# Experts of a two-layer trunk in chunks of 1024 columns: longer DMA rows, one split per load, 11 load buffers

## The chip, the cores and the metric

The kernel runs on one core of a Trainium2 chip. The metric is device time in microseconds (us) of one execution, the median of several runs. PE is TensorE (matmuls), PEld its weight loads, DVE is VectorE, ACT is ScalarE, POOL is GpSimd and SP is SyncE, which issues most transfers.

## The reference, cut to what matters

Two layers act on 256 tokens of width 1024: attention and a SwiGLU, then an HGRN2 mixer and a layer of experts. Only the experts change:

```python
def moe_swiglu(u, w_router, w_gate, w_up, w_down):
    t = u.reshape(B * S, D)                       # 256 x 1024, normalised
    logits = (t @ w_router).astype(F32)
    top_vals, top_idx = lax.top_k(logits, TOP_K)  # 2 of 8
    top_w = jax.nn.softmax(top_vals, axis=-1)
    gates = jnp.sum(jax.nn.one_hot(top_idx, N_EXPERTS, dtype=F32) * top_w[..., None], axis=1)
    out = jnp.zeros((B * S, D), F32)
    for e in range(N_EXPERTS):
        y = swiglu(t, w_gate[e], w_up[e], w_down[e]).astype(F32)
        out = out + gates[:, e:e + 1] * y
```

`swiglu` is `(silu(t @ w_gate) * (t @ w_up)) @ w_down`, with 3584 hidden columns per expert. All weights are float32: 44 MB for each expert, 352 MB of the 427 MB that the kernel reads.

## The kernel before

Products are made in a float32 format of reduced precision, so each operand is split into two parts, and a product is three matmuls: high x high, high x low, low x high (`mm3`, lines 101 to 103). Activations are split once per stage. Weights are split as they come: `load` (L83) takes a buffer of the pool `raws` (14 buffers of 1 MB) and issues one transfer on SP's queue; `split` (L88) makes `w_hi` on ACT by a copy and `w_lo` on DVE by a subtraction, into the pool `subs` (four buffers of each, 1024 columns wide). A load is split twice, by halves. The tile framework orders the instructions of each engine and puts in the waits; the order on an engine is fixed at build time.

The stages are attention (to 130 us), SwiGLU (to 340), HGRN2 (to 494) and the experts (to 1501). At the experts' start the tokens are normalised and transposed in two parts (`dense`), a router product of 24 small matmuls gives the logits (`route`, L1010), and DVE finds the two experts of each token (`sel`), its gate (`gw`) and its place in the list of each expert (`place`), for one token tile of 128 after the other. PE helps with sums over tokens (`pp`, L1036). `nh` and `nl` are the normalised tokens in two parts.

Each expert works on up to 128 tokens, gathered by a product with one-hot matrices (`one_hot`, L1053, `gather_pair`, L1060) for two experts at a time, e = 0, 2, 4, 6. An expert is seven jobs of 512 hidden columns. A job has a `gate` and an `up` (two loads each, 2 KB per row, 24 matmuls each), `hm` = the product of silu(gate) and up (L1111, DVE), a `turn` (four transposes, L1116, and the split of the result into `hh` on ACT and `hl` on DVE, L1120 and L1121) and a `down` (two loads of 4 KB rows, 24 matmuls into `pj`). `run_jobs` (L1208) interleaves them: gate of a job, turn of the one before, up, down of the one before. After an expert's last job `scatter` (L1194) multiplies the rows back to their tokens (L1202, L1203) and adds them to `h` (L1204). `FirstJob` runs its gate over all 256 tokens, 48 matmuls, while routing is under way; the result is gathered afterwards. `LastJob` ends half of the columns before the other, so that the output can leave early.

After all jobs the kernel counts the tokens of the fullest expert (L1254 to L1260); if there are more than 128, a second pass (L1262) does the rest. With these inputs it does not run, but the value has to be loaded by each engine (L1261) and the branch taken.

## Time and profile before

| | us |
|---|---|
| median of 3 runs | 1511.85 (1510.98 to 1514.09) |
| profiled execution, span | 1509.5 |
| of it, up to the first `up` matmul of the experts | 518.1 |
| of it, from there to the end of the last `down` matmul | 981.2 |
| of it, after that | 10.2 |
| PE busy | 1476.0 |
| DVE busy | 1243.6 |
| ACT busy | 1042.5 |

The span runs from the first to the last instruction that the profiler recorded in one execution. Busy time of an engine counts its own instructions; where an engine is busy almost all the time, the question is what it does and where its few gaps are, so the timeline and the waits matter more than the shares. The experts take the same pattern 56 times over, so one chunk's length times the number of chunks is most of the time. TensorE's granted clock was full through the experts.

### The profile page before, as it was taken

Reading aid. Unit: us, or ns where it says so; the run is one execution under the profiler, and the core shown is the slowest. Engines: PE = TensorE matmul, PEld = TensorE weight load, DVE = VectorE, ACT = ScalarE, POOL = GpSimd, SP = SyncE. Lnnn points to the kernel's source line nnn. Section 1 sums busy time; section 2 is a strip of 40 time slices with the busy share of each in tenths; the row PEclk is TensorE's granted clock in tenths of the full one; section 3 lists DMA queues with packets and bytes.
Section 4 is the critical chain, followed back from the end, with each engine's and each line's share of the span. In section 5 each row is a group of like instructions: output and inputs, shape, how many; then the busy total and the mean of one; then the engine's idle time right before and its main releaser. Section 6 shows DMA issues by size and latency. Waiting matters only on the chain.

```text
span 1509.5 us, 20242 instructions
## 1 busy us (share of the span) xinstructions
PE 1476.0 (98%) x7573; PEld 1228.3 (81%) x7573; DVE 1243.6 (82%) x1474; ACT 1042.5 (69%) x1293; POOL 14.9 (1%) x32
## 2 busy tenths in 40 slices
PE   7999999999999999999999999999999999999997
PEld 6787899998888788888888878888777887887885
DVE  7775655566767899999899998898889889889886
ACT  6655544445656788878778877777777777777774
POOL 1000000000000000000000000000000000000000
...
GB/s 312 368 117 112 137 185 195 178 185 182 140 156 125 142 376 363 373 364 362 360 325 377 377 329 362 371 315 362 362 369 345 361 355 326 362 363 343 365 260 31
DMA packets 208683, 429.85 MB, mean 285 GB/s; under 512 B 7290, under 2 KB 58530, under 8 KB 208578
## 3 DMA queue, kind: packets, MB, share of 16 engines
...
q8 instruction: 61, 1.00, 0.3%
...
## 4 chain that ended last, share of the span: by engine, by line
PE 92%; DVE 3%; ACT 2%; issue 1%; DMA 1%; POOL 0%; SPq 0%; ACTq 0%; DVEq 0%; POOLq 0%
PE acc L102 17%; PE acc L101 17%; PE acc L103 16%; PE pj L103 8%; PE pj L102 8%; PE pj L101 8%; PE pj L342 3%; PE pj L344 3%; PE pj L343 3%; DVE w_lo L91 2%; PE tp L1116 1%; PE pj L759 1%; PE pj L760 1%; PE pj L761 1%; PE acc L1069 1%
## 5 line engine op out<-in xcount | busy, mean ns | idle before, releaser
L91 DVE TENSOR_TENSOR w_lo<-raw,w_hi 128x1024 fp32r<-128x1024 f32 x810 | 958.5, 1221 | 163.4 <-ACT w_hi L91 146.1
L91 ACT ACTIVATE w_hi<-raw 128x1024 fp32r<-128x1024 f32 x810 | 835.8, 1058 | 275.8 <-PE acc L103 101.9
L102 PE MATMUL acc<-w_lo,xgh 128*128 128x512 f32 x904 | 357.2, 395 | 0.9
L101 PE MATMUL acc<-w_hi,xgh 128*128 128x512 f32 x904 | 355.9, 394 | 1.0 <-ACT xgh L294 1.0
L103 PE MATMUL acc<-w_hi,xgl 128*128 128x512 f32 x904 | 353.1, 391 | 0.0
L102 PEld LDWEIGHTS acc<-w_lo,xgh 128*128 128x128 f32 x904 | 169.7, 188 | 50.3 <-DVE w_lo L91 14.5
L101 PEld LDWEIGHTS acc<-w_hi,xgh 128*128 128x128 f32 x904 | 169.8, 188 | 36.4 <-ACT xgh L294 1.2
L103 PEld LDWEIGHTS acc<-w_hi,xgl 128*128 128x128 f32 x904 | 169.7, 188 | 33.8
L102 PE MATMUL pj<-w_lo,hh 128*128 128x512 f32 x448 | 177.1, 395 | 0.3
L103 PE MATMUL pj<-w_hi,hl 128*128 128x512 f32 x448 | 174.6, 391 | 0.3
L101 PE MATMUL pj<-w_hi,hh 128*128 128x512 f32 x448 | 161.1, 391 | 2.2 <-ACT hh L1120 1.7
L101 PEld LDWEIGHTS pj<-w_hi,hh 128*128 128x128 f32 x448 | 84.1, 188 | 21.5 <-ACT hh L1120 2.7
L102 PEld LDWEIGHTS pj<-w_lo,hh 128*128 128x128 f32 x448 | 84.1, 188 | 18.2 <-DVE w_lo L91 1.6
L103 PEld LDWEIGHTS pj<-w_hi,hl 128*128 128x128 f32 x448 | 84.1, 188 | 17.5 <-DVE hl L1121 1.1
L342 PE MATMUL pj<-xh,w_hi 128*128 128x256 f32 x320 | 90.8, 284 | 0.6 <-DVE hm L676 0.6
L344 PE MATMUL pj<-xh,w_lo 128*128 128x256 f32 x320 | 90.6, 283 | 0.0
L343 PE MATMUL pj<-xl,w_hi 128*128 128x256 f32 x320 | 90.6, 283 | 0.0
L1106 ACT ACTIVATE sg<-acc 128x512 f32<-128x512 f32 x55 | 33.0, 599 | 46.7 <-PE acc L103 46.7
L342 PEld LDWEIGHTS pj<-xh,w_hi 128*128 128x128 f32 x320 | 61.4, 192 | 1.2 <-DVE hm L676 0.8
L343 PEld LDWEIGHTS pj<-xl,w_hi 128*128 128x128 f32 x320 | 61.4, 192 | 0.4
L344 PEld LDWEIGHTS pj<-xh,w_lo 128*128 128x128 f32 x320 | 61.4, 192 | 0.0
L1120 ACT ACTIVATE hh<-tp 128x512 fp32r<-128x512 f32 x56 | 33.3, 595 | 40.4 <-PE pj L102 33.2
...
## 6 DMA issues: line engine op xcount, KB each, us to landing
...
```

Source lines behind the costliest of these rows:

```text
L91: split.last = nc.scalar.activation(hi, view, AF.Copy), nc.vector.tensor_sub(lo, view, f32(hi))
L101: nc.tensor.matmul(ps, lhsT=xh, rhs=wh, start=first, stop=False, skip_group_check=chk)
L102: nc.tensor.matmul(ps, lhsT=xh, rhs=wl, start=False, stop=False, skip_group_check=chk)
L103: nc.tensor.matmul(ps, lhsT=xl, rhs=wh, start=False, stop=last, skip_group_check=chk)
L342: nc.tensor.matmul(o, lhsT=wh[:, i, j], rhs=xh[:, k], start=k == 0 and j == 0, stop=False, skip_group_check=True)
L343: nc.tensor.matmul(o, lhsT=wh[:, i, j], rhs=xl[:, k], start=False, stop=False, skip_group_check=True)
L344: nc.tensor.matmul(o, lhsT=wl[:, i, j], rhs=xh[:, k], start=False, stop=k == KT - 1, skip_group_check=True)
L759: nc.tensor.matmul(o, lhsT=wh[:, k], rhs=xh[:, k], start=first, stop=False, skip_group_check=True)
L760: nc.tensor.matmul(o, lhsT=wh[:, k], rhs=xl[:, k], start=False, stop=False, skip_group_check=True)
L761: nc.tensor.matmul(o, lhsT=wl[:, k], rhs=xh[:, k], start=False, stop=last, skip_group_check=True)
L1106: nc.scalar.activation(self.sg, ps, AF.Silu)
L1120: nc.scalar.activation(self.hh, ptv, AF.Copy)
```

## The change

Experts are worked in jobs of 1024 columns, three per expert and one of 512 (the first of expert 0, the last of the others). A gate or up load covers two k-tiles of 1024 columns, in rows of 4 KB; a down load covers a pair of neighbouring hidden rows per partition, 8 KB, so the hidden columns of a job are permuted: `hm` is written (L1201) with even and odd columns apart, and the transposes read it so. Each load is one `Group` with one split of 128x2048 on ACT and one on DVE, and 12 matmuls. Splits are made three groups ahead (three `w_hi`, two `w_lo` buffers of a new pool `parts`), loads eleven ahead. The pool `subs` stays for the earlier stages only and is freed with them, and `parts` takes its place. The tables that route tokens were rewritten (`one_hot`, `pick`) to allow half-size lists, a form that the constant TWO = False leaves out; what stays of it are more table operations on DVE at the start and a transposition against an `order` matrix instead of the identity. The count of the fullest expert is made in `route`. The diff, cut to its core:

```diff
-NRAW = 14
+NRAW = 11
 NSUB = 4
+TWO = False
...
-    subs = ctx.enter_context(tc.tile_pool(name="subs", bufs=NSUB))
...
+    subs = early.enter_context(tc.tile_pool(name="subs", bufs=NSUB))
...
-    moe = ctx.enter_context(tc.tile_pool(name="moe", bufs=2))
+    moe = ctx.enter_context(tc.tile_pool(name="moe", bufs=1))
     mc = ctx.enter_context(tc.tile_pool(name="mc", bufs=1))
-
-    def slot_tiles(n):
-        """transposed rows in two parts: [feature, k-tile, row]"""
-        return [xgs.tile([P, KT, n], F32R, name=nm, tag=nm) for nm in ("xgh", "xgl")]
+    parts = ctx.enter_context(tc.tile_pool(name="parts", bufs=1))
...
+    lower = mc.tile([P, P], F32R, name="lower")
+    nc.vector.tensor_scalar(lower, ident, 0.0, None, op0=ALU.mult)
+    nc.vector.tensor_copy(lower[:, 0:HS], ident[:, HS:P])
+
+
+    even = mc.tile([P, P], F32, name="even")
+    nc.gpsimd.iota(it.rearrange("p (a b) -> p a b", b=2), pattern=[[1, HS], [0, 2]], base=1, channel_multiplier=0)
+    nc.vector.tensor_copy(even, it)
+    nc.vector.memset(even[:, 1:P:2], 0.0)
+    nc.vector.tensor_sub(even, even, slot1)
+    twice = mc.tile([P, P], F32, name="twice")
+    nc.vector.memset(twice[:, 0:HS], 0.0)
+    nc.vector.memset(twice[:, HS:P], -float(HS))
+
+    pi = moe.tile([P, 1], I32, name="pi", tag="pi")
+    nc.gpsimd.iota(pi, pattern=[[0, 1]], base=1, channel_multiplier=1)
+    place1 = mc.tile([P, 1], F32, name="place1")
+    nc.vector.tensor_copy(place1, pi)
+    step = mc.tile([P, 1], F32, name="step")
+    nc.vector.tensor_scalar(step, place1, float(HS), -float(P - 1), op0=ALU.is_gt, op1=ALU.mult)
+    nc.vector.scalar_tensor_tensor(step, place1, -1.0, step, op0=ALU.add, op1=ALU.add)
...
+            if t == NT - 1:
+                pc = bank("tp")
+                for u in range(NT):
+                    nc.tensor.matmul(pc[:, 0:NE], lhsT=ones, rhs=sel[:, u], start=(u == 0), stop=(u == NT - 1))
+                nc.vector.tensor_copy(count, pc[:, 0:NE])
+                if TWO:
+                    nc.vector.tensor_scalar(few, pc[:, 0:NE], float(HS), None, op0=ALU.is_le)
+                else:
+                    nc.vector.memset(few, 0.0)
+                nc.vector.tensor_reduce(out=cmax_i, in_=count, axis=AX.X, op=ALU.max)
...
+    def one_hot(e, small_slots, name):
+
+        slots = moe.tile([P, 2, P], F32, name="slots", tag="slots")
+        for i in range(2):
+            nc.vector.scalar_tensor_tensor(slots[:, i], small_slots, few[:, e + i:e + i + 1], slot1, op0=ALU.mult, op1=ALU.add)
+        oneh = moe.tile([P, NT, 2, P], F32R, name=name, tag=name, bufs=2)
         for t in range(NT):
-            nc.vector.tensor_tensor(out=oneh[:, t], in0=slot1[:, None, :].to_broadcast([P, 2, P]),
-                                    in1=place[:, t, e:e + 2, None].to_broadcast([P, 2, P]), op=ALU.is_equal)
+            nc.vector.tensor_tensor(out=oneh[:, t], in0=slots, in1=place[:, t, e:e + 2, None].to_broadcast([P, 2, P]),
...
+    class Group:
+
+        def __init__(self, pieces, arm, n):
+            self.pieces, self.arm, self.n = pieces, arm, n
+
+        def load(self):
+            self.raw = load([2048], self.pieces)
+
+        def split(self):
+            self.hi = parts.tile([P, 2048], F32R, name="w_hi", tag="w_hi", bufs=3)
+            self.lo = parts.tile([P, 2048], F32R, name="w_lo", tag="w_lo", bufs=2)
+            nc.scalar.activation(self.hi, self.raw, AF.Copy)
+            nc.vector.tensor_sub(self.lo, self.raw, f32(self.hi))
...
+            self.wd = weights[2].rearrange("(r p i) c -> p r (i c)", p=P, i=2)
...
+                return Group(lambda r: [(r.rearrange("p (k c) -> p k c", k=nk), w[:, k0:k0 + nk, self.c0:self.c0 + width])],
+                             arm, self.n)
+
+            return [begin] + [group(k0) for k0 in range(0, KT, nk)] + [lambda: self.low(box)]
...
+        def upped(self):
+
+            self.fold(self.pu)
+            self.hm = moe.tile([P, self.nb, 2, 2, P], F32, name="hm", tag="hm")
+            for b in range(self.nb):
+                nc.vector.tensor_mul(self.hm[:, b].rearrange("s a i p -> s a p i"),
+                                     self.pu["ps"][b].rearrange("s (a p i) -> s a p i", a=2, i=2),
+                                     self.sg[:, b].rearrange("s (a p i) -> s a p i", a=2, i=2))
...
+                return Group(lambda r: [(r, self.wd[:, self.c0 // 256 + a, :])], arm, self.n)
+
+            return [begin] + [group(a) for a in range(2 * self.nb)] + ([self.out] if self.last else [])
...
+    def run_jobs(jobs, fresh=lambda job: None):
+
+        todo = []
         prev = None
         for job in jobs + [None]:
-            if job and job.fresh:
-                job.fresh(job.shared)
-                if prev:
-                    prev.turn()
-                    prev.down()
-                    prev = None
+            into, rest = [], []
             if job:
-                job.gate()
+                into, rest = job.gate(), job.up()
+                rest[2:2] = [job.gated]
+                more = fresh(job)
+                if more:
+                    todo += more[:2] + ([prev.upped] if prev else []) + more[2:] + ([prev.turn] if prev else []) + into
+                elif prev:
+                    todo += into[:2] + [prev.upped] + into[2:] + [prev.turn]
+                else:
+                    todo += into
+                todo += rest
+            elif prev:
+                todo += [prev.upped, prev.turn]
             if prev:
-                prev.turn()
-            if job:
-                job.up()
-            if prev:
-                prev.down()
+                todo += prev.down()
             prev = job
 
+        groups = [i for i in todo if isinstance(i, Group)]
+        loaded = split_ = at = 0
+        for i in todo:
+            if isinstance(i, Group):
+                while split_ < min(at + 3, len(groups)):
+                    while loaded < min(split_ + NRAW, len(groups)):
+                        groups[loaded].load()
+                        loaded += 1
+                    groups[split_].split()
+                    split_ += 1
+                at += 1
+            i()
...
+    def pick(e, sh):
+        def fn():
+
+            sh["pick"] = one_hot(e, even, "low")
+            sh["oneh"] = one_hot(e, twice, "oneh")
+            for i in range(2):
+                at = small.tile([P, 1], F32, name="at", tag="at")
+                nc.vector.scalar_tensor_tensor(at, step, few[:, e + i:e + i + 1], place1, op0=ALU.mult, op1=ALU.add)
+                sh["order", i] = moe.tile([P, P], F32, name="order", tag="order", bufs=3)
+                nc.vector.tensor_scalar(sh["order", i], slot1, at, None, op0=ALU.is_equal)
+
+        return fn
...
+        widths = (1, 2, 2, 2) if e == 0 else (2, 2, 2, 1)
...
-    pc_ = bank("tp")
-    nc.tensor.matmul(pc_[:, 0:NE], lhsT=ones, rhs=sel[:, 0], start=True, stop=False)
-    nc.tensor.matmul(pc_[:, 0:NE], lhsT=ones, rhs=sel[:, 1], start=False, stop=True)
-    cmax = mc.tile([P, 1], F32, name="cmax")
-    nc.vector.tensor_reduce(out=cmax, in_=pc_[:, 0:NE], axis=AX.X, op=ALU.max)
-    cmax_i = mc.tile([P, 1], I32, name="cmax_i")
-    nc.vector.tensor_copy(cmax_i, cmax)
```

On DVE, where the previous stage ends, stood before, with the splits of the experts' first load (`raw_4991`) ahead of `ol`, the last part of the HGRN2 mixer, and `h0`, the residual:

```order
L915 TENSOR_TENSOR og_4746<-tp_4735,sg_4685 128x512
L916 TENSOR_TENSOR og_4746<-og_4746,hss_4748 128x512
L91 TENSOR_TENSOR w_lo_4994<-raw_4991,w_hi_4993 128x1024
L91 TENSOR_TENSOR w_lo_5010<-raw_4991,w_hi_5009 128x1024
L931 SCALAR_TENSOR_TENSOR ol_4772<-tp_4766,cols_88,oh_4771 128x512
```

and there now stands:

```order
L916 TENSOR_TENSOR og_4746<-tp_4735,sg_4685 128x512
L917 TENSOR_TENSOR og_4746<-og_4746,hss_4748 128x512
L932 SCALAR_TENSOR_TENSOR ol_4772<-tp_4766,cols_88,oh_4771 128x512
L310 TENSOR_TENSOR h0_77<-acc_3466,h0_77 128x512
L310 TENSOR_TENSOR h0_77<-acc_3467,h0_77 128x512
```

The two splits have gone from there.

Further on in DVE's order, at the routing, stood before (`nl` are the low parts of the tokens, `lT` and `lg` the logits, `m8` and `ix` the top two; `w_lo_5028` and `w_lo_5044` belong to the second load):

```order
L294 TENSOR_TENSOR xgl_4830<-tp_4878,xgh_4829 128x4x128
L1051 SCALAR_TENSOR_TENSOR nl0_4978<-hg0_4827,rs_4836,nh0_4900 128x512
L91 TENSOR_TENSOR w_lo_5028<-raw_5025,w_hi_5027 128x1024
L1051 SCALAR_TENSOR_TENSOR nl1_4983<-hg1_4828,rs_4863,nh1_4901 128x512
L1016 COPY lT_4930<-pj_4905 8x256
L1051 SCALAR_TENSOR_TENSOR nl1_4983<-hg1_4828,rs_4863,nh1_4901 128x512
L1022 TENSOR_SCALAR lg_4935<-tp_4932,rs_4836 128x8
L1022 TENSOR_SCALAR lg_4956<-tp_4932,rs_4863 128x8
L1024 MAX m8_4937<-lg_4935 128x8
L91 TENSOR_TENSOR w_lo_5044<-raw_5025,w_hi_5043 128x1024
L1026 MAX_INDEX ix_4939<-m8_4937,lg_4935 128x8
L1039 TENSOR_TENSOR dv_4949<-m8_4937 128x1
```

and now (`w_lo_5043` and `w_lo_5049` are the splits of the first and second load of the experts):

```order
L1050 MAX_INDEX ix_4963<-m8_4961,lg_4959 128x8
L1073 TENSOR_TENSOR dv_4973<-m8_4961 128x1
L1048 MAX m8_4982<-lg_4980 128x8
L1052 CAST ixf_4965<-ix_4963 128x8
L1128 TENSOR_TENSOR w_lo_5043<-raw_5020,w_hi_5042 128x2048
L1054 TENSOR_TENSOR s0_4967<-ei_4892,ixf_4965 128x16
L1050 MAX_INDEX ix_4984<-m8_4982,lg_4980 128x8
L1073 TENSOR_TENSOR dv_5001<-m8_4982 128x1
L1056 TENSOR_TENSOR sel_4923<-s0_4967 128x8
L1077 TENSOR_SCALAR gw_4924<-s0_4967,g2_4975 128x8
L1052 CAST ixf_4986<-ix_4984 128x8
L1128 TENSOR_TENSOR w_lo_5049<-raw_5022,w_hi_5048 128x2048
```

The first split of the experts stands behind the logits of both token tiles, and the second behind `sel` of the first tile.

In the middle of an expert DVE had, per chunk of 512 columns, one `hm` and one `hl` between splits of 1024:

```order
L91 TENSOR_TENSOR w_lo_9522<-raw_9519,w_hi_9521 128x1024
L91 TENSOR_TENSOR w_lo_9532<-raw_9519,w_hi_9531 128x1024
L1111 TENSOR_TENSOR hm_9516<-acc_9471,sg_9469 128x512
L91 TENSOR_TENSOR w_lo_9544<-raw_9541,w_hi_9543 128x1024
L91 TENSOR_TENSOR w_lo_9554<-raw_9541,w_hi_9553 128x1024
L91 TENSOR_TENSOR w_lo_9578<-raw_9575,w_hi_9577 128x1024
L91 TENSOR_TENSOR w_lo_9588<-raw_9575,w_hi_9587 128x1024
L91 TENSOR_TENSOR w_lo_9600<-raw_9597,w_hi_9599 128x1024
L1121 TENSOR_TENSOR hl_9571<-tp_9565,hh_9570 128x512
L91 TENSOR_TENSOR w_lo_9610<-raw_9597,w_hi_9609 128x1024
```

and now, per job of 1024 columns, two `hm` between splits of 2048 (`hq` holds what `hh` and `hl` held):

```order
L1128 TENSOR_TENSOR w_lo_6301<-raw_6066,w_hi_6300 128x2048
L1128 TENSOR_TENSOR w_lo_6319<-raw_6084,w_hi_6318 128x2048
L1201 TENSOR_TENSOR hm_6446<-acc_6275,sg_6295 128x2x128x2
L1128 TENSOR_TENSOR w_lo_6337<-raw_6102,w_hi_6336 128x2048
L1201 TENSOR_TENSOR hm_6446<-acc_6276,sg_6295 128x2x128x2
L1128 TENSOR_TENSOR w_lo_6357<-raw_6120,w_hi_6356 128x2048
L1128 TENSOR_TENSOR w_lo_6375<-raw_6138,w_hi_6374 128x2048
```

An operation of the old size now stands singly between splits of twice the size.

On PE, the end of the program stood before as follows (L1202 and L1203 scatter, L1255 and L1256 count the tokens):

```order
L1202 MATMUL tp_13716<-yh_13707,back_13644 128x512
L1203 MATMUL tp_13711<-yl_13708,back_13644 128x512
L1203 MATMUL tp_13716<-yl_13708,back_13644 128x512
L1255 MATMUL tp_13721<-sel_4902,ones_84 128x8
L1256 MATMUL tp_13721<-sel_4902,ones_84 128x8
L1261 TENSOR_LOAD cmax_i_13726
L1262 COMPARE_AND_BRANCH
```

and now:

```order
L1140 MATMUL pj_11804<-w_lo_12251,hq_12268 128x512
L1140 MATMUL pj_11804<-w_hi_12250,hq_12268 128x512
L1348 MATMUL tp_12321<-y_12318,back_12279 128x512
L1348 MATMUL tp_12326<-y_12318,back_12279 128x512
L1349 MATMUL tp_12321<-y_12318,back_12279 128x512
L1349 MATMUL tp_12326<-y_12318,back_12279 128x512
L1434 TENSOR_LOAD cmax_i_4928
L1435 COMPARE_AND_BRANCH
```

The count is gone from the end, and the load of its result stands straight behind the last scatter.

## Rows read from the trace of the kernel before

**Rows 1.** The page's busy time, share of the span and instructions, by engine.

```profile
PE 1476.0 (98%) x7573; PEld 1228.3 (81%) x7573; DVE 1243.6 (82%) x1474; ACT 1042.5 (69%) x1293; POOL 14.9 (1%) x32
```

**Rows 2.** Timeline of PE in the experts: start us, us, engine, line, operation, count.

```profile
560.60 0.39 PE L101 MATMUL acc<-w_hi,xgh 128*128 128x512 f32 x1
...
562.41 0.40 PE L103 MATMUL acc<-w_hi,xgl 128*128 128x512 f32 x1
```

**Rows 3.** Timeline of DVE: two pairs of neighbouring `hm`, early and late.

```profile
603.24 0.68 DVE L1111 TENSOR_TENSOR hm<-acc,sg 128x512 f32<-128x512 f32 x1
...
620.05 0.68 DVE L1111 TENSOR_TENSOR hm<-acc,sg 128x512 f32<-128x512 f32 x1
...
1061.27 0.69 DVE L1111 TENSOR_TENSOR hm<-acc,sg 128x512 f32<-128x512 f32 x1 [0.63 <-PE acc L103]
...
1078.37 0.69 DVE L1111 TENSOR_TENSOR hm<-acc,sg 128x512 f32<-128x512 f32 x1 [0.63 <-PE acc L103]
```

**Rows 4.** All loads of line 85, 440 to 1500 us: from issue to landing.

```profile
DMA to landing us min/median/max: 4.4/7.4/10.6
```

**Rows 5.** Waits of the load queue, 560 to 1509: total us, times, longest.

```profile
SPq L85 <- DVE w_lo L91: 766.6, 307, 7.1
```

**Rows 6.** Waits of all engines, 600 to 1500 us: the weight load's.

```profile
PEld acc L102 <- DVE w_lo L91: 14.5, 36, 0.6
```

**Rows 7.** The page's costliest groups: the splits (busy us, mean ns, idle before).

```profile
L91 DVE TENSOR_TENSOR w_lo<-raw,w_hi 128x1024 fp32r<-128x1024 f32 x810 | 958.5, 1221 | 163.4 <-ACT w_hi L91 146.1
L91 ACT ACTIVATE w_hi<-raw 128x1024 fp32r<-128x1024 f32 x810 | 835.8, 1058 | 275.8 <-PE acc L103 101.9
```

**Rows 8.** One stretch: busy time of the engines, granted clock, DMA share, GB/s.

```profile
550.00:600.00 50.00, 50.00 (x228) 41.40 (x227) 46.43 (x43) 40.45 (x43) 0.00 (x0) 1.00 1.01 364
```

**Rows 9.** Single lines: duration ns min/median/max, first and last start.

```profile
L1111 DVE TENSOR_TENSOR hm<-acc,sg x56: 680/691/692, 524.6 to 1485.6; 128x512 f32<-128x512 f32 x56
...
L1204 DVE SCALAR_TENSOR_TENSOR h<-tp,gw,h x32: 739/743/753, 643.6 to 1502.1; 128x512 f32<-128x512 f32 x32
```

**Rows 10.** Timeline of DVE at the start of the experts.

```profile
487.05 2.35 DVE L91 TENSOR_TENSOR w_lo<-raw,w_hi 128x1024 fp32r<-128x1024 f32 x2
...
500.14 0.68 DVE L294 TENSOR_TENSOR xgl<-tp,xgh 128x512 fp32r<-128x512 f32 x1
...
500.74 0.74 DVE L1051 SCALAR_TENSOR_TENSOR nl<-hg,rs,nh 128x512 fp32r<-128x512 f32 x1
...
501.40 1.22 DVE L91 TENSOR_TENSOR w_lo<-raw,w_hi 128x1024 fp32r<-128x1024 f32 x1
...
503.20 0.41 DVE L1016 COPY lT<-pj 8x256 f32<-8x256 f32 x1
...
504.55 1.21 DVE L91 TENSOR_TENSOR w_lo<-raw,w_hi 128x1024 fp32r<-128x1024 f32 x1
...
509.66 0.16 DVE L1032 TENSOR_TENSOR sel<-s 128x8 f32<-128x8 f32 x1
```

**Rows 11.** Timeline of PE at the start of the experts.

```profile
512.27 0.39 PE L103 MATMUL acc<-w_hi,xgl 128*128 128x512 f32 x1
...
512.50 0.63 PE L1069 MATMUL acc<-oneh,nh 128*128 128x256 f32 x4
...
518.12 0.40 PE L101 MATMUL acc<-w_hi,xgh 128*128 128x512 f32 x1
```

**Rows 12.** Timeline at the end, and two single lines (duration ns, start).

```profile
1499.05 0.39 PE L103 MATMUL pj<-w_hi,hl 128*128 128x512 f32 x1
...
1500.85 0.73 PE L1203 MATMUL tp<-yl,back 128*128 128x512 f32 x2
...
1503.10 0.15 DVE L1260 CAST cmax_i<-cmax 128x1 int32<-128x1 f32 x1
...
L1261 PEldq TENSOR_LOAD <-cmax_i x1: 803/803/803, 1503.4 to 1503.4; - x1
...
L1262 PEldq COMPARE_BRANCH  x1: 4108/4108/4108, 1504.3 to 1504.3; - x1
```

297 lines of the change are left out of this document (173 added, 124 removed).

## The prediction

> **What bounds the kernel now.** I read the page first: TensorE (PE) is busy 98% of the span [rows 1], so the sum goes by what PE must do and by where PE stands still. Two thirds of the span, from 494 us, are the experts. There one 512-column matmul starts every 0.227 us (eight steps from 560.60 to 562.41, [rows 2]), so 12 matmuls, the work that one 1 MB load feeds, take 2.72 us. The next view is the distance between two `hm` rows, one chunk: 16.81 us early, 17.10 us late [rows 3]; 72 matmuls and four transposes of 0.109 make 16.76. Early chunks are thus at PE's floor, and about 23 late ones (from 880 us on, those inside an expert) lose 0.29 each, 6.7 us in all. From the first `up` matmul at 518.12 to the end of the last `pj` matmul, 1499.28, is 981.2 us; 4008 matmuls x 0.2267, 224 transposes and the gathers and scatters between experts come to some 971, so about 10 us are stalls: 6.7 late chunks, 3 or so at the ends of experts.
>
> The memory system is not what PE waits for. A MoE load lands 7.4 us after issue, at most 10.6 [rows 4], and the load queue itself waited 766.6 us for `w_lo`, that is for buffers that VectorE (DVE) still reads [rows 5]. What PE waits for is the other half of a split: the weight load of line 102 waited 14.5 us on `w_lo` [rows 6]. The splits cost 1.221 us on DVE and 1.058 on ScalarE (ACT) for 1024 columns [rows 7]. DVE is the second busiest engine.
>
> **The change part by part.**
>
> *Rows of 4 and 8 KB.* These shorten transfers that nothing waits for. 50 us of the middle moved 364 GB/s with all DMA engines busy [rows 8], because loads run ahead until buffers are full; PE needs 1 MB per 2.72 us only. I cost this at nothing, and its cover is the lead of the queue. With 11 buffers instead of 14, three stay with splits, eight are ahead, 8 x 2.72 = 22 us against a landing of at most 10.6. The stages before have smaller loads and lose three buffers too; I put 0 there, bound 0 to +2.
>
> *One split of 2048 instead of two of 1024.* DVE 1024 columns 1.221 [rows 7], 512 columns 0.691 [rows 9], so 1.04 ns per column, and a split of 2048 is an estimated 2.29 us (in a row of splits the pace is some 0.08 less), for ACT about 2.0. Both lie under 2.72. With two `w_lo` buffers a split may begin when the group two back has read its last `w_lo`, and has about 3.0 to 3.2 us until PE wants it: a slack of 0.6 to 0.9 us. `hm` (two operations of 0.69) and `hq` (the same kind) stand singly between splits in the new order, so each fits into that slack. The late 0.29 us per chunk, which came where `w_lo` followed `w_hi` too closely, then has no reason. The gain is 6.7 at best; I keep back 1 for the 24 pairs of `hm`: **-5.7** (range -6.7 to +1).
>
> *Start of the experts.* Before, the first load's splits ran while PE was still in the previous stage: two `w_lo` at 487.05, then at 501.40 and 504.55, between them the small work of the routing [rows 10]. PE could push the 48 gate matmuls of the first job between the router's: the last ran at 512.27, the gather began at 512.50 and `up` at 518.12 [rows 11]. Now the split buffers take the memory of the earlier stages' pool, and no split precedes the last matmul there; on DVE the first stands behind all four `xgl`, some ten new small operations for the slot tables, four `nl`, `lT`, both `lg` and the first index, and the second stands ahead of the second tile's `sel`. By rows: the last `xgl` starts at 500.14, ends its pace at 500.74; ten small ones at about 0.1 make 1.0; four `nl` at 0.66 (500.74 to 501.40) make 2.6; `lT`, `lg`, `MAX` about 0.7 and the index 0.35; then 2.29 of split: 507.7. PE has done two gate matmuls by then and does seven more, then its queue stands at the matmul that needs `sel` of the second tile, which comes after 0.7 of small work, a second split of 2.2 and 0.6 of small work: 511.3. It needs about 0.3 to get going; 39 matmuls x 0.227 = 8.8 bring it to 520.5, the gather and its companions the same 5.6 (512.50 to 518.12) as before: `up` at 526.1 instead of 518.12, **+8.0**. The bounds: +5 if DVE gets to the first split 3 us earlier because ACT feeds it sooner, +10 if the small operations take twice that.
>
> *Ends of experts.* In the new order, eight operations of about 0.62 to 0.74 (two `yl`, four `h`, two `hm`; [rows 9]) lie among four splits: 4 x 2.2 + 5.2 = 14.0 us of DVE. PE has four groups, 10.9, and 2.1 of its own (two transposes, eight scatter matmuls): 13.0. Short by 1.0, part of which the lead of a split covers; I take 0.8 x 7 = 5.6. The routing tables of the next two experts (`pick`) are about a dozen operations where two one-hots stood, some 2.3 us of DVE per pair; a third of it shows, 0.8 x 3 = 2.3. Together 7.9 against 3 before: **+4.8** (0 if DVE's lead covers all, +12 if nothing is covered).
>
> *The end.* Before, the count of the fullest expert was made after the last row: `cmax_i` at 1503.10, then PE's load of it 0.80 and its branch 4.11 us, which ends at 1508.4 [rows 12]. Now the count is made in the routing, so PE can load it when its last matmul (from 1500.85, 0.73) is through: 1501.6 instead of 1503.4. I take **-2.0** (0 if the last transfer of the output ends the span instead). SyncE's load of it moves too, to right after the thirteenth load of the experts; what is queued behind it are loads whose buffers are not free sooner, so 0.
>
> *The permuted `hm`.* Its write steps 512 bytes between neighbours, so that a down load can bring row pairs. No row of before writes so. The ends: 0.69 as now, or 1.22 as for twice the columns [rows 7, 9]. I take the first, as reads and the number of elements are the same; the second is a rival. [...]
>
> Sum: +8.0 - 5.7 + 4.8 - 2.0 = +5.1. From 1509.5 that is a span of 1514.6; the median of the runs shown lies 2.35 above the profiled span, so the forecast is **1517 us**.
>
> **The rivals.** *Slower still, by the stride:* at 1.22 each, two `hm` cost 1.1 more per job of 1024 columns. A slack of 0.6 to 0.9 is used up by then, some 0.4 to 0.6 us reach PE; 24 such jobs give +10 to +14, so 1527 to 1531. For it: nothing in the trace, except that VectorE has little slack. Against: the four elements after each other come back to the same two places.
>
> *Not slower:* the ends of experts and tables cost nothing because splits are one group ahead whenever PE does transposes, scatters or gathers. It decides at a shortage of 0.6 us, within the slack above; my shortage of 1.0 is near to it. Then -3 instead of +4.8: 1514.6 - 7.8 = 1506.8, median about 1509, and 1506 if the start loses only 5. For it: early chunks run at the floor already with finer splits. Against: one buffer of `w_lo` ahead instead of three.
>
> *Memory becomes the bound:* with 11 buffers the landing would have to exceed 22 us for a wait. If the 8 KB rows landed that late, ACT's splits would wait on loads. Nothing speaks for it at a maximum of 10.6; a run of ten waits of 1 us would give 1527.
>
> **How the numbers follow.** My forecast, a start later by 5 to 10 us and small change elsewhere, 0.5: 1512 to 1522. Not slower, 0.27: 1503 to 1510. Stride, 0.18: 1522 to 1531. Memory, 0.05. The range 1505 to 1529 leaves out the ends of the second and third. A measurement tells 0.2% from no change, 3.0 us, thus 1508.8 and 1514.9 are the bounds: faster 0.22 (most of the not-slower case), same 0.25 (its rest and the low end of the forecast), slower 0.53.
>
> **What would show it.** The start: the first `up` matmul of the experts near 526, `sel` of the second tile behind the second split. The steady part: distances of the pairs of `hm` near 33.6 within late experts, and 2.2 to 2.3 us for a split. The ends: PE's weight loads waiting on `w_lo` right after scatters. The stride: the duration of the `hm` operation. The end: no `cmax` after the last `h`, the branch nearer to it. I am wrong most of all if the start is hidden, which `up` at 520 would show, or if DVE, at more than 90% busy, is the bound all through.

## The result, and the profile after

The changed kernel takes 1556.92 us (median of 4 runs, 1554.66 to 1560.35) against 1511.41 of the kernel before beside it: a ratio of 1.0305, interval 1.0286 to 1.0323. It is slower, as forecast, but by 45 us, not by 5. The profiled execution has a span of 1558.6 us against 1509.5, that is +49.1. That execution took 1560.35 us, the longest of the four, so the parts below add up to some 3.5 us more than the medians differ by.

The page of the changed kernel, span and busy times, answers to [rows 1]:

```profile
span 1558.6 us, 19593 instructions
...
PE 1505.8 (97%) x7573; PEld 1237.6 (79%) x7573; DVE 1244.7 (80%) x1189; ACT 994.0 (64%) x957; POOL 15.7 (1%) x34
```

PE ran the same 7573 instructions and was busy 30 us longer. DVE's time is unchanged, ACT's is less. So the time did not go into more work on DVE, the engine that the prediction watched.

Both traces are divided at three starts of matmuls: the last one of the HGRN2 mixer, the first `up` of the experts, and the last `pj`.

| us | before | after | difference | predicted |
|---|---|---|---|---|
| until the last HGRN2 matmul starts | 493.97 | 496.68 | +2.7 | 0 |
| start: from there to the first `up` | 24.15 | 37.42 | +13.3 | +8.0 |
| body: from there to the last `pj` | 980.9 | 1015.7 | +34.8 | -0.9 |
| from there to the end of the span | 10.48 | 8.8 | -1.7 | -2.0 |

The first line varies by itself: runs of the changed kernel with the same code up to there had 490.91 to 496.86. The body is what went wrong. The first half of its explanation is in a timeline that answers to [rows 2] (PE, changed kernel; columns as there; between the two rows lie 14 starts):

```profile
544.83 0.39 PE L1140 MATMUL acc<-w_lo,xg 128*128 128x512 f32 x1
...
548.33 0.40 PE L1140 MATMUL acc<-w_lo,xg 128*128 128x512 f32 x1
```

Fifteen steps take 3.50 us, 0.2333 each, with nothing waited for and the granted clock at 1.00 (544.8 to 548.7 us). In [rows 2] a step was 0.2263, at the same granted clock. The mean over the body, of all neighbouring matmuls less than 0.26 us apart, is 233.44 ns against 227.92. Times 4008 matmuls that is 22.1 us.

The second half is gaps. Steps longer than 0.5 us exceed a normal step by 21.4 us together in the body of the changed kernel (26 of them, most near 1.0) and by 5.1 before (13), so +16.3. Both make 38.4 of the 34.8; the -3.6 left is with gaps shorter than that, which I did not sort.

### The profile page after: what moved, and what is told of

Its sections match the earlier page's. It is cut to its first block, busy times and chain, and to the rows that moved or that the text cites. A ratio compares the mean times of both kernels' runs of the same rounds, so it can differ in the third digit from the quotient of the medians.

```text
span 1558.6 us, 19593 instructions
## 1 busy us (share of the span) xinstructions
PE 1505.8 (97%) x7573; PEld 1237.6 (79%) x7573; DVE 1244.7 (80%) x1189; ACT 994.0 (64%) x957; POOL 15.7 (1%) x34
## 4 chain that ended last, share of the span: by engine, by line
PE 86%; DVE 8%; ACT 3%; DMA 2%; issue 1%; POOL 0%; SPq 0%; DVEq 0%; ACTq 0%; POOLq 0%
PE acc L1140 35%; PE pj L1140 20%; DVE w_lo L1128 4%; PE acc L102 3%; PE acc L103 3%; PE acc L104 3%; PE pj L343 2%; PE pj L344 2%; PE pj L345 2%; ACT w_hi L1127 1%; PE pj L102 1%; PE pj L104 1%; PE pj L103 1%; PE tp L1225 1%; PE pj L760 1%
## 5 line engine op out<-in xcount | busy, mean ns | idle before, releaser
L1128 DVE TENSOR_TENSOR w_lo<-raw,w_hi 128x2048 fp32r<-128x2048 f32 x336 | 764.8, 2289 | 117.7 <-PE acc L1140 35.4
L1127 ACT ACTIVATE w_hi<-raw 128x2048 fp32r<-128x2048 f32 x336 | 641.4, 1918 | 202.9 <-PE acc L1140 114.8
L1140 PE MATMUL acc<-w_hi,xg 128*128 128x512 f32 x1776 | 568.8, 396 | 0.0
L1140 PEld LDWEIGHTS acc<-w_hi,xg 128*128 128x128 f32 x1776 | 333.2, 188 | 77.7 <-DVE xg L1114 0.2
L1140 PE MATMUL acc<-w_lo,xg 128*128 128x512 f32 x888 | 354.9, 400 | 15.8 <-DVE w_lo L1128 14.9
L1140 PE MATMUL pj<-w_hi,hq 128*128 128x512 f32 x896 | 287.6, 396 | 0.8 <-ACT hq L1228 0.7
L92 DVE TENSOR_TENSOR w_lo<-raw,w_hi 128x1024 fp32r<-128x1024 f32 x138 | 168.6, 1223 | 106.8 <-ACT w_hi L92 103.2
L92 ACT ACTIVATE w_hi<-raw 128x1024 fp32r<-128x1024 f32 x138 | 145.7, 1058 | 145.6 <-PE pj L344 71.3
L1140 PEld LDWEIGHTS pj<-w_hi,hq 128*128 128x128 f32 x896 | 168.8, 189 | 40.1 <-ACT hq L1228 1.1
L1140 PE MATMUL pj<-w_lo,hq 128*128 128x512 f32 x448 | 181.5, 405 | 0.7 <-DVE w_lo L1128 0.6
L1201 DVE TENSOR_TENSOR hm<-acc,sg 128x512 f32<-128x512 f32 x56 | 58.7, 1107 | 2.7 <-PE acc L1140 2.7
```

Of the source, the lines that this page charges most:

```text
L92: split.last = nc.scalar.activation(hi, view, AF.Copy), nc.vector.tensor_sub(lo, view, f32(hi))
L1127: nc.scalar.activation(self.hi, self.raw, AF.Copy)
L1128: nc.vector.tensor_sub(self.lo, self.raw, f32(self.hi))
L1140: nc.tensor.matmul(ps, lhsT=x_, rhs=w_, start=first and i == 0, stop=last and i == len(xs) - 1, skip_group_check=True)
L1201: nc.vector.tensor_mul(self.hm[:, b].rearrange("s a i p -> s a p i"), self.pu["ps"][b].rearrange("s (a p i) -> s a p i", a=2, i=2), self.s ...
```

## The experiments

In the tables and texts, "step" is that mean distance of matmuls in the body, "stalls" that sum of gaps in us, counted on to PE's last matmul (22.3 in the changed kernel, 6.7 before), "start" and "body" are the stretches above. Unless the text says otherwise, an experiment is an edit of the changed kernel, and its time is that of one execution.

### What makes a matmul step 233 instead of 228 ns

First the buffers and the layout. One more `w_lo` buffer, one load buffer less for it:

```diff
-NRAW = 11
+NRAW = 10
-            self.lo = parts.tile([P, 2048], F32R, name="w_lo", tag="w_lo", bufs=2)
+            self.lo = parts.tile([P, 2048], F32R, name="w_lo", tag="w_lo", bufs=3)
```

> The changed kernel with three w_lo buffers instead of two and ten load buffers instead of eleven; nothing else. In the changed kernel a 512-column matmul starts every 233.4 ns in the experts, before every 226.7 to 228. Theory A, that matmuls are slow because w_lo is finished only just ahead of its use: the step returns to 227 to 228 ns, 21 us in all, and the seventeen waits of 1.1 to 1.4 us for w_lo go with it, another 15 us: a span near 1522. Theory B, that the step comes from something else (where the operands lie, how they are laid out, the larger transfers): the step stays at 233 ns, only the waits go: near 1543.

Measured: 1555.26 us, step 233.45, stalls 22.7, body 1014.9. Neither the step nor the stalls moved, so one more `w_lo` ahead mends neither.

High and low parts of the operands apart from each other, as `xgh` and `xgl` were before, rather than interleaved:

```diff
-            sh["xg"] = xgs.tile([P, KT, 2, 2, P], F32R, name="xg", tag="xg")
+            sh["xg"] = xgs.tile([P, 2, KT, 2, P], F32R, name="xg", tag="xg")
...
-            self.hq = moe.tile([P, self.nb, 4, 2, P], F32R, name="hq", tag="hq")
+            self.hq = moe.tile([P, 2, self.nb, 4, P], F32R, name="hq", tag="hq")
```

> The changed kernel with the high and the low part of the weights' partner (xg, hq) in two planes, as before the change, instead of one behind the other per 128 columns; nothing else. Theory C, that the slow matmul step of 233.4 ns comes from that interleaved layout: 227 to 228 ns, a span near 1537. If the layout does not matter: 233 ns and 1558.

Measured: 1557.01 us, step 233.44, body 1017.2. Not the layout inside a tile either.

Next the place of the tiles. A pool has a fixed place in each partition, and the change moved nearly all of them. One line moved the splits' pool:

```diff
+    parts = ctx.enter_context(tc.tile_pool(name="parts", bufs=1))
     (ahead of the pool xgs, where it stood behind it)
```

> The changed kernel with the pool of the splits (parts) created ahead of the other pools of the experts, so that w_hi and w_lo lie where the earlier stages' splits lay (122464 to 163423 in each partition) instead of at 186656 to 227615, and the experts' activations behind them; nothing else. Theory D, that matmuls start every 233.4 ns instead of 227 because of where their operands lie: the step falls to 227 to 228 ns, some 21 us, a span near 1536. The rival, that place does not matter: 233 ns and 1553 to 1558.

Measured: 1544.62 us, body 1006.0, and a step of 229.56 that is a mixture. The groups by line of PE (560 to 1480 us; busy us, mean ns of one, idle before) show it, here of the changed kernel:

```profile
L1140 PE MATMUL acc<-w_hi,xg 128*128 128x512 f32 x1608 | 515.5, 396 | 0.0
...
L1140 PE MATMUL pj<-w_hi,hq 128*128 128x512 f32 x810 | 259.5, 396 | 0.0
```

and of the kernel with the moved pool:

```profile
L1140 PE MATMUL acc<-w_hi,xg 128*128 128x512 f32 x1642 | 517.4, 391 | 0.0
...
L1140 PE MATMUL pj<-w_hi,hq 128*128 128x512 f32 x805 | 257.5, 395 | 0.0
```

The mean here is that of the profile's records of one matmul. They overlap, so it is longer than a step, but it differs by the same 5 ns. The gate and up products (`acc`) became short, step 227.8; the down products (`pj`) stayed long, 233.1. What differs is where the two operands of a matmul start in the partition, as the build places them, in bytes. The moving operand is the 512 columns of `w_hi` or `w_lo`, the stationary one the 128 columns of activations (`xgh`, `xg`, `hh` or `hq`); the difference is activations minus `w_hi`:

| kernel | `w_hi` | activations of `acc` | difference mod 256 | step | activations of `pj` | difference mod 256 | step |
|---|---|---|---|---|---|---|---|
| before | 140832 | 179744 | 0 | 228 | 211488 | 0 | 228 |
| changed | 186656 | 122464 | 64 | 233 | 167040 | 96 | 234 |
| pool moved | 122464 | 163424 | 0 | 227.8 | 208000 | 32 | 233.1 |

Neither operand's own offset decides it. `w_hi` starts at 32 modulo 256 before, with a short step, and in the changed kernel, with a long one; `xg` starts at 96 in the changed kernel, long, and with the pool moved, short. So the theory: a step is short where the moving operand (weights) and the stationary one (activations) start at equal offsets within some power of two. Three kernels test it. The first makes all offsets equal by padding; the second makes the `acc` pair differ by 256 and the `pj` pair by 128:

```diff
+    moe.tile([P, 120], F32, name="pad", tag="pad")     (second kernel: 24)
+    mc.tile([P, 88], F32, name="padc")                 (second kernel: 120)
```

> The changed kernel with 480 and 352 unused bytes per partition put into two pools, so that w_hi, w_lo, xg and hq all begin at the same offset within 512 bytes (96); nothing else. Theory E, that a matmul starts every 227 instead of 233 ns only if its two operands lie at equal offsets within some power of two of at most 512 bytes (so it was for all matmuls of the kernel before, and for acc but not pj in the run with the splits low): 227 to 228 ns for acc and pj, some 21 us off, a span of 1534 to 1538. Rival F, that it takes the low place of the splits itself: 233 ns and 1553 to 1558.

> The changed kernel with other unused bytes, so that w and xg differ by 256 within 512 bytes and w and hq by 128; nothing else. Under theory E this tells what the offsets must agree in: if within 128 bytes, acc and pj both start every 227 ns; if within 256, acc 227 and pj 233; if within 512, both 233.

Measured, first kernel: 1543.58 us, body 998.8, that is 16.9 less than the changed kernel's, step 227.87 with both products short (227.7 and 228.3). The count of steps gives 22.3; stalls rose by 1.8, and the rest went to shorter gaps. Second: 1544.59 us, `acc` 228.1, `pj` 232.6. Groups by line as above, of the first and then of the second:

```profile
L1142 PE MATMUL acc<-w_hi,xg 128*128 128x512 f32 x1645 | 518.3, 391 | 0.0
...
L1142 PE MATMUL pj<-w_hi,hq 128*128 128x512 f32 x816 | 257.1, 390 | 0.0
```

```profile
L1142 PE MATMUL acc<-w_hi,xg 128*128 128x512 f32 x1642 | 517.9, 391 | 0.0
...
L1142 PE MATMUL pj<-w_hi,hq 128*128 128x512 f32 x805 | 256.9, 394 | 0.0
```

Equal within 256 bytes was enough (228.1), a difference of 128 was not (232.6). The third kernel goes the other way: the kernel before, with 64 unused bytes ahead of its operands but behind its split buffers.

```diff
+    gains.tile([P, 16], F32, name="pad", tag="pad")
```

> The kernel before with 64 unused bytes per partition between the splits' pool and the pools of the activations; nothing else. Theory E: all its matmuls with 512 columns start every 233 instead of 227 ns, in the experts some 4000 x 5.5 ns = 22 us, in the stages before 3 to 8 us more where PE is the bound: a span of 1530 to 1540. Theory F: 227 ns, 1510 to 1513.

Measured: 1529.62 us, 18 more than before, step 233.38. The stages ahead of the experts have the long step too (233), but it costs nothing there: the last HGRN2 matmul starts at 494.10 instead of 493.97. Groups by line again, of the kernel before and then of this one:

```profile
L101 PE MATMUL acc<-w_hi,xgh 128*128 128x512 f32 x837 | 329.2, 393 | 0.0
...
L101 PE MATMUL pj<-w_hi,hh 128*128 128x512 f32 x416 | 148.8, 391 | 1.5 <-ACT hh L1120 1.5
```

```profile
L102 PE MATMUL acc<-w_hi,xgh 128*128 128x512 f32 x822 | 327.5, 398 | 0.0
...
L102 PE MATMUL pj<-w_hi,hh 128*128 128x512 f32 x408 | 148.5, 396 | 1.5 <-ACT hh L1121 1.5
```

Nothing else in that kernel changed: the `w_hi` and `w_lo` buffers stay where they were, the activations and all tiles behind them lie 64 bytes further, and the body is 999.1 instead of 980.9. The cause is shown in both directions. Neighbours are not it: in the changed kernel, matmuls after 1519.7, when the last load had landed, and matmuls beside which neither DVE nor ACT ran, had 233.5 and 233.9. Why an unequal start costs 5 to 6 ns per step is open.

### The order on ACT

In the changed kernel the waits of all engines from 600 to 1550 us (total us, times, longest) have these rows; the third answers to [rows 6]:

```profile
ACT sg L1190 <- PE acc L1140: 45.9, 28, 3.1
DVE w_lo L1128 <- ACT w_hi L1127: 33.9, 23, 2.5
PEld acc L1140 <- DVE w_lo L1128: 29.2, 34, 1.4
```

PE waits on `w_lo`, `w_lo` on `w_hi`, both 23 to 34 times, near once per job (there are 29), and ACT itself waits 28 times on `acc`, at `sg`. Before, `sg` waited as long in all, and `w_lo` longer, but in more and shorter pieces (600 to 1500 us):

```profile
ACT sg L1106 <- PE acc L103: 45.2, 50, 1.7
DVE w_lo L91 <- ACT w_hi L91: 39.5, 72, 1.8
```

So it is not the sum of these waits that grew, but the single one, for `sg` from 0.9 to 1.6 us. The timeline of one job shows the three as a chain:

```profile
850.16 0.60 ACT L1190 ACTIVATE sg<-acc 128x512 f32<-128x512 f32 x1 [2.98 <-PE acc L1140]
...
850.66 1.91 ACT L1127 ACTIVATE w_hi<-raw 128x2048 fp32r<-128x2048 f32 x1
...
852.59 4.58 DVE L1128 TENSOR_TENSOR w_lo<-raw,w_hi 128x2048 fp32r<-128x2048 f32 x2 [2.41 <-ACT w_hi L1127]
...
854.94 0.50 PE L1140 MATMUL acc<-w_lo,xg 128*128 128x512 f32 x1 [0.85 <-DVE w_lo L1128]
```

ACT is idle for 2.98 us with `sg` at the head of its queue, which needs the last gate matmul. Behind it stands a `w_hi` whose load has landed and whose buffer is free. It begins 2.98 us late, DVE waits 2.41 for it, PE stands still for 0.85. The edit lets one split pass `sg`:

```diff
+            his.append(nc.scalar.activation(self.hi, self.raw, AF.Copy))
...
-            for b in range(self.nb):
-                nc.scalar.activation(self.sg[:, b], self.pg["ps"][b], AF.Silu)
+            with tc.issue_after(his[-2].ins):
+                for b in range(self.nb):
+                    nc.scalar.activation(self.sg[:, b], self.pg["ps"][b], AF.Silu)
```

> The changed kernel with ACT's silu of the gate (sg) held behind the split of the second group of up, nothing else. In the changed kernel ACT stands still for about 3 us with sg at the head of its queue, waiting for the gate's last matmul, while a w_hi whose load and buffer are there stands behind it; w_lo follows late and PE waits 1.0 us, once per job of 1024 columns in most experts. Theory: those waits (some sixteen of 1.0 us) go: a span of 1538 to 1543. Rival, that w_hi was waiting for its buffer or load anyway: the waits stay and the span stays at 1553 to 1558.

Measured: 1539.41 us, body 1004.1 (-11.6), stalls 11.8 instead of 22.3. The same waits (600 to 1540 us):

```profile
PEld acc L1142 <- DVE w_lo L1130: 16.0, 24, 1.4
ACT sg L1193 <- PE acc L1142: 15.1, 28, 0.9
DVE w_lo L1130 <- ACT w_hi L1129: 10.0, 12, 1.1
```

`sg` still waits 28 times, 0.5 each instead of 1.6, and PE's waits are back near the sum of [rows 6] (16.0 against 14.5), though the longest is still 1.4. Of the 26 long steps in the body 10 are gone. So ACT, at 64% busy, was on the path in about ten of the jobs, at 1.0 us each.

### The permuted `hm`

The single line of `hm` in the changed kernel (duration ns, minimum, median, maximum) answers to [rows 9]:

```profile
L1201 DVE TENSOR_TENSOR hm<-acc,sg x56: 1073/1104/1136, 541.9 to 1529.6; 128x512 f32<-128x512 f32 x56
```

The same 512 elements per partition take 1.104 us instead of 0.691. The experiment writes them in natural order, which makes a down load bring two rows of 4 KB per partition instead of one of 8 KB:

```diff
-            self.wd = weights[2].rearrange("(r p i) c -> p r (i c)", p=P, i=2)
+            self.wd = weights[2].rearrange("(r i p) c -> p r i c", p=P, i=2)
...
-                nc.vector.tensor_mul(self.hm[:, b].rearrange("s a i p -> s a p i"),
-                                     self.pu["ps"][b].rearrange("s (a p i) -> s a p i", a=2, i=2),
-                                     self.sg[:, b].rearrange("s (a p i) -> s a p i", a=2, i=2))
+                nc.vector.tensor_mul(self.hm[:, b].rearrange("s a i p -> s (a i p)"), self.pu["ps"][b], self.sg[:, b])
```

> The changed kernel with hm written in its natural order, so without the 512-byte step, and the down loads as two rows of 4 KB per partition instead of one of 8 KB. Theory: the write's step made hm last 1.107 us instead of 0.69; it returns to 0.69, 56 x 0.42 = 23 us of DVE time, and those waits of PE for w_lo that stand behind two hm operations (about a third of the seventeen) go: 5 to 10 us, a span of 1548 to 1553. The rival, that hm is slow because two of them read PSUM while PE writes there: it stays at 1.1 and the span at 1558. If rows of 8 KB in flight made matmuls slow, their step would fall below 233 ns here.

Measured: 1550.46 us, body 1009.0 (-6.7), step unchanged at 233.43, stalls 18.3. The line of `hm`:

```profile
L1201 DVE TENSOR_TENSOR hm<-acc,sg x56: 680/691/692, 538.5 to 1519.5; 128x512 f32<-128x512 f32 x56
```

The gap of PE that follows two `hm` fell from 1.12 to 0.47. It shows six times, about once per expert, and not in every job, so that is 4.0 us, as the stalls have it; the other 2.7 are in shorter gaps. 56 x 0.413 = 23 us of DVE were saved, 6.7 of them reached the end. The 8 KB rows that the stride bought brought nothing that could be seen in exchange.

### The buffers and the end, alone

The kernel before with 11 load buffers (`NRAW = 11`):

> The kernel before with 11 load buffers instead of 14, nothing else. In the changed kernel the last matmul of the HGRN2 stage ended 2 us or so later than before, in stages whose code is the same. Theory, that fewer buffers cost it: the last matmul of that stage comes 1 to 3 us later here too, and the experts lose nothing: a span of 1510 to 1513. Rival, that it is variation between executions: 494.0 as before.

Measured: 1514.13 us, one run; body 983.3 instead of 980.9, the last HGRN2 matmul at 494.2 instead of 493.97, step 228.01. At most 2.4 us, near what one execution differs from the next.

The kernel before with the count of the fullest expert made in `route`, five rounds:

```diff
+            if t == NT - 1:
+                pc_ = bank("tp")
...
+                nc.vector.tensor_reduce(out=cmax_i, in_=count, axis=AX.X, op=ALU.max)
...
-    nc.vector.tensor_copy(cmax_i, cmax)
```

> The kernel before with the count of the fullest expert moved into the routing, as the change does, nothing else. Theory, as in the prediction: PE loads the value as soon as its last matmul is through, 1.5 to 2 us earlier: a median 1.5 to 2 us (0.10 to 0.13%) under the kernel before. Rival, that the output's last transfer or SyncE's own load ends the span: no change, or a loss where SyncE's early load holds up transfers behind it.

Measured: 1510.49 against 1510.93 us, ratio 0.9998 (0.9989 to 1.0007). In the trace the stretch from the last `pj` to the end is 9.3 instead of 10.5 us, so the step is real there, but 1.2 us is less than this measurement can tell from nothing.

### The start, and all repairs together

At the start, PE's timeline in the changed kernel is this; the last row answers to the last of [rows 11]:

```profile
506.55 0.28 PE L104 MATMUL pj<-both,gTl 128*8 128x256 f32 x1
...
511.54 0.54 PE L1140 MATMUL acc<-w_lo,both 128*128 128x512 f32 x1 [3.91 <-DVE w_lo L1128]
...
522.25 0.40 PE L1140 MATMUL acc<-w_lo,both 128*128 128x512 f32 x1
...
534.10 0.39 PE L1140 MATMUL acc<-w_hi,xg 128*128 128x512 f32 x1
```

DVE's timeline has the first split and the second tile's `sel`, which answers to the last of [rows 10]:

```profile
509.21 2.27 DVE L1128 TENSOR_TENSOR w_lo<-raw,w_hi 128x2048 fp32r<-128x2048 f32 x1
...
514.74 0.15 DVE L1056 TENSOR_TENSOR sel<-s 128x8 f32<-128x8 f32 x1
```

And the stretches of the start (busy us of PE, PEld, DVE, ACT, POOL, granted clock, DMA share, GB/s):

```profile
507.00:512.00 5.00, 0.75 (x4) 0.42 (x4) 5.00 (x20) 2.28 (x5) 0.00 (x0) 0.99 0.00 0
512.00:522.00 10.00, 10.00 (x30) 8.26 (x30) 6.61 (x24) 0.10 (x2) 0.00 (x0) 0.50 0.58 211
522.00:534.00 12.00, 11.31 (x64) 9.61 (x63) 10.99 (x21) 8.54 (x10) 0.00 (x0) 1.00 0.43 142
```

PE did 0.75 us of work in 5, waiting for the first `w_lo`, and then ran ten microseconds at a granted clock of 0.50. It did 30 instructions in these ten; by an estimate from the two clocks of these rows, 0.50 and 1.00, it would have done about twice as many at 1.00, so some 5 us went there. In the kernel before, PE had no such wait and kept a clock of 1.00:

```profile
507.00:512.00 5.00, 5.00 (x26) 4.22 (x25) 4.24 (x20) 3.20 (x7) 0.00 (x0) 1.00 0.84 283
```

ACT had made its half of the first split long before. It was DVE's order that held the other half back to 509.21:

```profile
497.15 1.91 ACT L1127 ACTIVATE w_hi<-raw 128x2048 fp32r<-128x2048 f32 x1 [1.32 <-issue]
```

The experiment puts the first two splits ahead of the routing on ACT and DVE:

```diff
+        while split_ < 2:
+            while loaded < min(split_ + NRAW, len(groups)):
+                groups[loaded].load()
+                loaded += 1
+            groups[split_].split()
+            split_ += 1
+        first()
...
-    route()
-    run_jobs(jobs, fresh)
+    run_jobs(jobs, fresh, route)
```

> The changed kernel with the splits of the first two loads of the experts put ahead of the routing in the program, nothing else. In the changed kernel PE stood still from 507.6 to 511.5 us, then ran at half the granted clock until 521.7, and the first up matmul came at 534.1. Theory: the wait was for w_lo behind small work on DVE; with the splits earlier PE does not stand still, keeps its full clock and the up matmul comes near 524: 10 us off, a span near 1548. Rival: the splits now hold up the last xgl and the routing, so that PE waits for those instead: less than 4 us off.

Measured: 1550.64 us, start 29.8 instead of 37.4, body 1016.1. The clock stayed at 1.00:

```profile
510.00:522.00 12.00, 10.83 (x63) 9.09 (x61) 10.68 (x26) 8.88 (x10) 0.00 (x0) 1.00 0.39 131
```

The start is still 5.6 us longer than before. First the repairs of start, `sg` and `hm` were joined:

> The changed kernel with three of the edits together: hm in natural order, the first two splits ahead of the routing, and sg behind the second split of up. If the parts add up: 10 for the start, 7 for hm, 15 for sg off 1558.6, a span near 1527. What is left over the kernel before is then the slower step of the matmuls, 21 us. If the waits are the same ones, told twice: 1535 to 1540.

Measured: 1536.23 us, start 29.8, body 999.1, step 233.44, stalls 7.8. The body fell by 16.6; `sg` and `hm` alone had given 11.6 and 6.7, 18.3 together.

Then the pads of the equal offsets were added, three rounds:

> The changed kernel with the three edits of c1 (hm in natural order, two splits ahead of the routing, sg behind a split) and the unused bytes of the same-offset run. Theory: 1534.5 less 21 us, a span of 1511 to 1516, within 0.3% of the kernel before; the order of the queues, the placement and the stride of hm then account for the whole loss, and the chunks of 1024 columns as such for none of it. Rival: above 1520.

Measured: 1513.51 us, ratio 1.0016 (1.0006 to 1.0025), body 978.6, step 227.66, stalls 8.2. With the other two losses repaired, the pads gave 20.5 in the body, near the 22 of the count. All that the change lost in the body is found: it is 2.4 less than before's 980.9. What keeps this kernel slower is the start, 29.7.

Are the routing tables the reason? They were taken out as far as `TWO = False` leaves them unused (`lower`, `even`, `twice`, `step`, `slots`, `order` and the second one-hot), so that tables and gather are those of the kernel before; five rounds:

> The four edits of c2 and without the tables and table operations that the switched-off small lists need (lower, even, twice, place1, step, few, slots, order, a second one-hot): one-hots straight from the places, transposes with the identity, offsets of w, xg and hq again equal within 256 bytes (32). Theory: in c2 the first up matmul still comes 6 us later than in the kernel before, because some 15 small operations of DVE, 3 to 4 us, stand ahead of the splits, sel and the gather; without them it comes 3 to 4 us earlier (near 521) and the ends of expert pairs lose a further 1 to 2: a median of 1507 to 1510, 0.1 to 0.3% under the kernel before. Rival, that the start is late because the splits cannot begin before the earlier stage's pool is free: up stays near 524 and the median at 1512 to 1514.

Measured: 1513.91 us, ratio 1.0018 (1.0009 to 1.0027), start 30.3. By the medians the tables are not the reason. (In the profiled execution PE ran 3.4 us of this start at 0.50, a mean clock of 0.83 from 500 to 510 us, which by an estimate from the two clocks cost up to 1.7; the four repairs had 1.00 there.) Or is it the memory, which the first split gets from the earlier stages only when they are through? The last kernel gives the first group buffers of its own, and takes two load buffers for it:

```diff
-NRAW = 11
+NRAW = 9
+    pre = ctx.enter_context(tc.tile_pool(name="pre", bufs=1))
...
+            if first:
+                self.hi, self.lo = [pre.tile([P, 2048], F32R, name=n, tag=n) for n in ("w_hi", "w_lo")]
```

> The c3 kernel with one pair of split buffers for the first load only, taken ahead of all stages (16 KB per partition, so 9 load buffers instead of 11), so that this split need not wait until the earlier stages' pool is free. Theory, after c3 has shown that the tables are not what makes the start late: it is the place of the first split; it now runs before the HGRN2 stage ends, PE weaves the gate's matmuls among the router's as in the kernel before, and the first up matmul comes near 519 instead of 524.8, 5 to 6 us off: a median of 1507 to 1510. Rival, that nine load buffers bring waits for loads, 2 to 10 us in the body: no gain.

Measured: 1507.58 against 1511.24 us in five rounds, ratio 0.9977 (0.9967 to 0.9987). The start is 25.1, body 977.3, step 227.64. The first split now ran on ACT at 426.78, inside the HGRN2 stage; in the kernel without tables it began at 494.99. PE's first matmul of the gate on a `w_lo` starts at 497.37 with no wait for it, instead of at 502.73 after 1.80 of waiting:

```profile
502.73 0.73 PE L1114 MATMUL acc<-w_lo,both 128*128 128x512 f32 x1 [1.80 <-DVE w_lo L1102]
```

The first `up` on PE in the last kernel:

```profile
519.25 0.39 PE L1118 MATMUL acc<-w_hi,xg 128*128 128x512 f32 x1
```

So the wait for memory was the rest of the start but for 1.0 us, and this kernel takes 0.2% less than the one before.

All runs in one table:

| kernel | time us | start | body | step ns | stalls |
|---|---|---|---|---|---|
| before | 1511.41 | 24.15 | 980.9 | 227.92 | 6.7 |
| changed | 1556.92 | 37.4 | 1015.7 | 233.44 | 22.3 |
| one more `w_lo` buffer | 1555.26 | 33.6 | 1014.9 | 233.45 | 22.7 |
| parts apart | 1557.01 | 35.2 | 1017.2 | 233.44 | 22.2 |
| `hm` in order | 1550.46 | 35.9 | 1009.0 | 233.43 | 18.3 |
| two splits early | 1550.64 | 29.8 | 1016.1 | 233.43 | 22.3 |
| splits' pool moved | 1544.62 | 32.9 | 1006.0 | 229.56 | 24.1 |
| `sg` behind a split | 1539.41 | 33.7 | 1004.1 | 233.43 | 11.8 |
| equal offsets | 1543.58 | 37.3 | 998.8 | 227.87 | 24.1 |
| offsets 256 and 128 | 1544.59 | 33.5 | 1005.3 | 229.58 | 24.0 |
| three repairs | 1536.23 | 29.8 | 999.1 | 233.44 | 7.8 |
| four repairs | 1513.51 | 29.7 | 978.6 | 227.66 | 8.2 |
| and no tables | 1513.91 | 30.3 | 978.1 | 227.56 | 8.4 |
| and own first buffer | 1507.58 | 25.1 | 977.3 | 227.64 | 8.9 |
| before, 11 load buffers | 1514.13 | 24.1 | 983.3 | 228.01 | 7.2 |
| before, count early | 1510.49 | 24.5 | 980.8 | 227.89 | 6.0 |
| before, 64 bytes shifted | 1529.62 | 24.1 | 999.1 | 233.38 | 5.9 |

## Why the prediction was right in sign and wrong in size

**The step that failed** is the one that is not there. The prediction worked out 2.72 us for twelve matmuls from [rows 2] and used it for before and after alike; a term for the matmul step itself is missing from the sum. In the changed kernel twelve matmuls took 2.80 us. The missing term was about 22 us by the count of steps, 16.9 by the kernel with equal offsets alone, 20.5 with the other losses of the body repaired, and 18 in the kernel before when shifted. Neither the order of instructions nor the diff shows it: the duration of a matmul was taken as fixed by its shape, and the change moved its operands.

**The steady part (-5.7)** had the wrong sign besides. It looked for slack on DVE only, between two `w_lo`. ACT was left out since its splits "lie under 2.72", but in the job shown above ACT stood idle for 2.98 us with `sg` at the head of its queue, and the `w_hi` behind it came late. With one split per load, a whole load's split (1.918 us) stands behind an `sg` that waits for the gate to end. That cost 11.6. DVE's own slack was about as calculated: a split took 2.289 us on DVE and 1.918 on ACT (predicted 2.29 and about 2.0), on the page of the changed kernel that answers to [rows 7]:

```profile
L1128 DVE TENSOR_TENSOR w_lo<-raw,w_hi 128x2048 fp32r<-128x2048 f32 x336 | 764.8, 2289 | 117.7 <-PE acc L1140 35.4
...
L1127 ACT ACTIVATE w_hi<-raw 128x2048 fp32r<-128x2048 f32 x336 | 641.4, 1918 | 202.9 <-PE acc L1140 114.8
```

**The permuted `hm`** was costed at the wrong one of its two ends. It took 1.104, near the upper bound of 1.22, and 0.691 again in order, so the rival was right about the stride; its price was 6.7 us, not 10 to 14: the rival took 0.4 to 0.6 for each of 24 jobs, and the gap behind `hm` showed in six places, where it shrank by 0.65.

**The ends of experts (+4.8)** and the gain of coarser splits were not told apart by a run. Together they were to make -0.9; in the three kernels with everything else repaired, the body is 2.4 to 3.7 us below before's in one execution of each. Of that, 1.0 to 1.4 us is a slightly shorter step (227.56 to 227.66 against 227.92). Chunks of 1024 columns are thus worth 1 to 3 us when nothing else is in the way.

**The start (+8.0)** was right in where the first split stands and wrong in what follows it. The split began at 509.21, 12.5 us behind the last HGRN2 matmul (predicted about 505.4, thus 11.4 behind it). PE had two gate matmuls done by then, as predicted, but stood still for this `w_lo` and not for `sel` of the second tile. It went on at 511.54 and had no gap in the 16 us after. That 511.3 plus 0.3 was predicted is luck: it was another wait, and the stage ahead ended 2.7 later. The 0.3 to get going was an estimate; PE went on 0.06 behind the end of this `w_lo` (511.48). There were 46 matmuls left, not 39, and the prediction counted them at the full clock. How long PE then ran at 0.50 differs between executions. In the 16 us behind PE's wait for the first `w_lo` the mean granted clock was 0.68 in the changed kernel and in the one with equal offsets (start 37.4 and 37.3), 0.70 with `hm` in order (35.9), 0.75 with the parts apart (35.2), 0.85 with three `w_lo`, with offsets of 256 and 128 and with `sg` behind a split (33.6, 33.5 and 33.7). Take off what each lost there, by an estimate from these clocks (16 x 0.32 = 5.1, 4.8, 4.0, 2.4), and 31.1 to 32.3 remain, 7.0 to 8.2 above before. The kernel with the splits' pool moved does not fit in: its wait was 2.91 instead of 3.9, its clock 0.82, and its 32.9 less 2.9 leaves 30.0. By this estimate the rest of the +13.3 is the clock, for which the prediction had no term. Its +8.0 thus stands as a number, its reasons only in part. The tables were no part of it that the medians show, while the wait for the earlier stages' memory, which the prediction names, was worth about 5 once the splits stood early (30.3 against 25.1; 6 by the medians).

**The end (-2.0)** was -1.7 in the changed kernel and -1.2 alone.

**Rows of 4 and 8 KB, eleven buffers (0 each)**: a load landed a little sooner (median 6.3 us after issue, before 7.4), and the queue waited for buffers 81% of the time, as before, as all loads from 440 to 1550 us and the queue's waits (530 to 1560; before 560 to 1509) show; they answer to [rows 4] and [rows 5]:

```profile
DMA to landing us min/median/max: 4.6/6.3/9.0
```

```profile
SPq L86 <- DVE w_lo L1128: 834.9, 318, 8.1
```

No wait from 600 to 1550 us that ends with a transfer was longer than 1.0 us, and the kernel that is faster than both has nine buffers. That rival is out.

**Not slower** would have been true of the idea, not of this code: with its four losses repaired, and without the tables and the 8 KB rows, it is 0.2% faster.
